# Encoder block on one core: the first four key tiles in one pass over K, weights of the next group cast before the last K step, head norms with a lag of two

## The chip, the core and the metric

The kernel runs on one core of a Trainium2 chip. A core has a matrix engine (TensorE, PE in the profile), VectorE (DVE), ScalarE (ACT), GpSimd (POOL) and SyncE (SP), which here issues nearly all transfers. Each engine works through its own instructions in program order and waits on semaphores for the others. The metric is the time of one execution on the device in microseconds; a time is the median of several executions.

## What is computed

One encoder layer over 1024 tokens of 1024 channels, in float32:

```
h = rms_norm(x, norm1_g)
a, gate, q, k, v = split(h @ w_in)
conv_out = silu(layer_norm(depthwise_conv(a * sigmoid(gate))))
q, k = rms_norm per head of 64 (q), rms_norm per head of 64 (k)
attn_out = neighbourhood_attention(q, k, v, rpb)
x = x + concat(conv_out, attn_out) @ w_out
h = rms_norm(x, norm2_g)
x = x + (silu(h @ w_gate) * (h @ w_up)) @ w_down
```

## The kernel before

The order of the work is written out by hand; no scheduler moves anything. Every large product is taken as three float32r matmuls (`mac`, lines 110 to 114): an operand is split into a rounded high half and the low rest; high by high, high by low and low by high are summed in PSUM. The split of weights is `split` (line 103): ScalarE casts (line 104), POOL or VectorE subtracts (line 108).

Weights come as chunks in a fixed list: wk0 to wk3 (the key projection's four K steps of 256 channels), then ag10, ag00, ag11 and so on for the gated convolution. `issue` (line 134) sends the next chunk from SP into one of three raw buffers, `take` (line 144) splits a chunk, `take_parts` (line 156) hands the split out in pieces.

The input is used transposed: `load_xt` (line 215) brings a quarter of x transposed, for the first or second 256 tokens of a half (FIRST, SECOND) or for all 512, and `h_split` (line 256) scales it by the norm's weight and splits it (ScalarE line 259, VectorE line 260) into hT. The row norm 1/rms itself, r1, is not multiplied in there; `stats1` (line 276) computes it for one tile of 128 tokens, odd tiles by bn_stats on VectorE, even tiles by a square on ScalarE, with a square root on ScalarE and a reciprocal on VectorE behind each. `r_rows` (line 284) spreads r1 of four tiles along rows with four transposes on TensorE (line 289), which the gate and value steps of the convolution group need.

A key tile z1t is 24 matmuls of 128x512. `head_post` (line 420) is what follows it: square (ScalarE, line 368), sum (VectorE, 369), square root (ScalarE, 375), reciprocal (VectorE, 380), scaling (VectorE, 382), and `head_T` (line 386): four transposes on TensorE (389) and a copy to kT on ScalarE (396). head_T is put in a list, `woven`, behind empty entries (seven, line 426); after each `mac` of a later group one entry is taken from the list. `step` (line 408) keeps the post-work of a group until the next group has been issued.

The start of the kernel, lines 505 to 541: tiles 0 and 1 go through the four K steps together, with wk split just ahead; then the second 256 tokens are split, statistics of tiles 0 and 1 follow, then tile 2, statistics of tiles 2 and 3, the split of ag10 (line 533), and tile 3 with the head norms of the tiles before it. Then come r_rows(0) and the groups gl00, gl01 (first half of the tokens) and gl10, gl11 (`glu_step`, line 430).

Of the kernel before, what the change touches and what calls it, by code (L numbers as in the profile page):

```python
# [12 lines left out]
P = 128  # L13
D = 1024
S = 1024
KB = D // P
# [51 lines left out]
def build(ctx, tc, a):  # L68
    nc = tc.nc
    pe, act, dve, pool = nc.tensor, nc.scalar, nc.vector, nc.gpsimd  # L70
# [5 lines left out]
    def T(tag, shape, bufs, name, dt=F32):  # L76
        return sb.tile(shape, dt, tag=tag, bufs=bufs, name=name)

    def G(name, dt=F32):
        return T("G", [P, 1024], 22, name, dt)  # L80

    def R(name):
        return T("R", [P, 1024], 3, name)

    def H(name, dt=F32):
        return T("H", [P, 4096], 6, name, dt)

    def ST(name, dt=F32):
        return T("st", [P, 512], 5, name, dt)

    def SM(name, n=8):
        return T("sm", [P, 8], 16, name)[:, :n]

    def mm(name):
        return ps.tile([P, 512], F32, tag="mm", bufs=4, name=name)

    def tp(name):
        return ps.tile([P, 512], F32, tag="tp", bufs=2, name=name)
# [4 lines left out]
    def split(hi, lo, src, sub=(pool,)):  # L103
        act.copy(hi, src)  # L104
        n = src.shape[-1] // len(sub)
        for i, eng in enumerate(sub):
            sl = slice(i * n, (i + 1) * n)
            eng.tensor_tensor(*[w[..., sl] for w in (lo, src, hi.bitcast(F32))], OP.subtract)  # L108

    def mac(acc, l, r, start, stop):  # L110
        (lh, ll), (rh, rl) = l, r
        pe.matmul(acc, lh, rh, start=start, stop=False, skip_group_check=True)  # L112
        pe.matmul(acc, lh, rl, start=False, stop=False, skip_group_check=True)  # L113
        pe.matmul(acc, ll, rh, start=False, stop=stop, skip_group_check=True)  # L114


    woven = []
# [10 lines left out]
    chunks, raws = [], {}  # L128
    pos = [0, 0]
# [4 lines left out]
    def issue():  # L134
        if pos[0] < len(chunks):
            src, name, _, _ = chunks[pos[0]]
            raws[pos[0]] = R(name + "r")
            d = raws[pos[0]]
            if len(src.shape) == 3:
                d = d.rearrange("p (k m) -> p k m", k=src.shape[1])  # L140
            nc.sync.dma_start(d, src)
            pos[0] += 1

    def take(n=1, ahead=True):
        for _ in range(n):
            i = pos[1]
            while pos[0] <= i:
                issue()
            _, _, dst, sub = chunks[i]
            hi, lo = dst()  # L150
            split(hi, lo, raws.pop(i), sub)
            pos[1] += 1
            if ahead and pos[0] < i + 4:
                issue()
# [22 lines left out]
    wn = {n: [] for n in range(3)}  # L177
# [29 lines left out]
    hT = [[H(f"hT{h}{w}", F32R).rearrange("p (k s) -> p k s", s=512) for w in range(2)] for h in range(2)]  # L207
    x_t, xr = {}, {}
    FIRST, SECOND, ALL = slice(0, 256), slice(256, 512), slice(0, 512)

    def load_x(t):
        x_t[t] = G(f"x{t}")
        nc.sync.dma_start(x_t[t], a["x"][t * P:(t + 1) * P, :])

    def load_xt(h, kp, sl):
        if (h, kp) not in xr:
            xr[h, kp] = G(f"xt{h}{kp}").rearrange("p (k s) -> p k s", s=512)
        nc.sync.dma_start(xr[h, kp][:, :, sl], a["xt"][h, kp][:, :, sl])

    for kp in range(4):  # L220
        load_xt(0, kp, FIRST)
        if kp < 3:
            issue()
    ones = ST("ones")[:, :P]
    ident = T("ident", [P, P], 1, "ident")
    par = T("par", [P, 146], 1, "par")
    nc.scalar.dma_start(par, a["par"])
    g1 = par[:, 0:8]
    dwk = par[:, 8:132].rearrange("p (c t) -> p c t", t=CW)
    dwb, lng, lnb = par[:, 132:136], par[:, 136:140], par[:, 140:144]  # L230
# [3 lines left out]
    warm = SM("warm", 1)  # L234
    act.activation(warm, eps, AF.Sqrt)
    pool.memset(ones, 1.0)
    pool.affine_select(ident, ones, pattern=[[-1, P]], compare_op=OP.is_equal, fill=0.0,
                       base=0, channel_multiplier=1)
    qgs = T("qgs", [P, 1], 1, "qgs")
# [16 lines left out]
    def h_split(h, k, sl):  # L256
        src = xr[h, k // 2][:, k % 2, sl]
        hi, lo = [w[:, k, sl] for w in hT[h]]
        act.activation(hi, src, AF.Copy, scale=g1[:, k:k + 1])
        dve.scalar_tensor_tensor(lo, src, g1[:, k:k + 1], hi.bitcast(F32), OP.mult, OP.subtract)  # L260
# [15 lines left out]
    def stats1(t):  # L276
        ss, scale = (bn_sum if t % 2 else sq_sum)(t)
        sd = SM(f"sd1{t}", 1)
        act.activation(sd, ss, AF.Sqrt, bias=eps, scale=scale)
        dve.reciprocal(r1[:, t:t + 1], sd)  # L280
# [11 lines left out]
    def nat(n, t):  # L292
        z = mm(f"z{n}{t}")
        h, o = divmod(t * P, 512)
        for k in range(KB):
            mac(z, [q[:, k, o:o + P] for q in hT[h]],
                [q[:, (k % 2) * 512:(k % 2) * 512 + 512] for q in wn[n][k // 2]], k == 0, k == KB - 1)
            weave()
        return z
# [56 lines left out]
    def pump(n):  # L356
        for _ in range(n):
            if not next(conv, False):
                return
# [4 lines left out]
    def head_sq(n, t, z):  # L364
        sq, ss = ST(f"sq{n}{t}"), SM(f"s{n}{t}")
        r = r1[:, t:t + 1]
        if n == 1 and t < 4:
            act.activation(sq, z, AF.Square, scale=r)
            dve.tensor_reduce(ss, sq.rearrange("p (h d) -> p h d", d=HD), mybir.AxisListType.X, OP.add)
        else:  # L370
            for h in range(NH):
                act.activation(sq[:, h * HD:(h + 1) * HD], z[:, h * HD:(h + 1) * HD], AF.Square, scale=r,  # L372
                               accum_out=ss[:, h:h + 1])
        sd = SM(f"d{n}{t}")
        act.activation(sd, ss, AF.Sqrt, bias=eps, scale=1.0 / HD)
        return sd

    def head_scale(n, t, z, sd):
        r = SM(f"r{n}{t}")
        dve.reciprocal(r, sd)  # L380
        zn = ST(f"zn{n}{t}")
        dve.scalar_tensor_tensor(zn.rearrange("p (h d) -> p h d", d=HD), z.rearrange("p (h d) -> p h d", d=HD),
                                 r1[:, t:t + 1], r[:, :, None].to_broadcast([P, NH, HD]), OP.mult, OP.mult)
        return zn

    def head_T(n, t, zn):
        pt = tp(f"zt{n}{t}")
        for c in range(4):
            pe.transpose(pt[:, c * P:(c + 1) * P], zn[:, c * P:(c + 1) * P], ident)
        if n == 0:  # L390
            q5 = qT.rearrange("p c (h b i j) -> p c h b i j", h=2, b=4, j=16)
            p5 = pt.rearrange("p (c i b j) -> p c i b j", c=4, i=2, j=16)
            for i in range(2):
                act.activation(q5[:, :, t // 4, :, 2 * (t % 4) + i, :], p5[:, :, i], AF.Copy, scale=qgs)
        else:
            act.activation(kT[:, :, t * P:(t + 1) * P], pt.rearrange("p (c s) -> p c s", s=P), AF.Copy, scale=kg)
# [9 lines left out]
    pend = []  # L406
# [10 lines left out]
            pump(n_taps)  # L417
        side()

    def head_post(n, t, z):  # L420
        def f(n_taps):
            sd = head_sq(n, t, z)
            pump(2 + {(1, 5): 3, (0, 1): 2}.get((n, t), 0))
            zn = head_scale(n, t, z, sd)
            pump(1)
            woven.extend([lambda: None] * 7)
            woven.append(lambda: head_T(n, t, zn))
        return f

# [71 lines left out]
    def project(n, t, post):  # L501
        z = nat(n, t)
        step(post(n, t, z))

    zs = [mm(f"z1{t}") for t in range(2)]
    for kp in range(4):
        parts = []
        take_parts(parts, 2, dve)
        for j in range(2):
            h_split(0, 2 * kp + j, FIRST)  # L510
            parts[j]()
        if kp == 0:
            for q in range(4):
                load_xt(0, q, SECOND)
            load_x(0)
            load_x(1)
        if kp == 2:
            load_x(2)
            load_x(3)
        for j in range(2):  # L520
            for t in range(2):
                k = 2 * kp + j
                mac(zs[t], [q[:, k, t * P:(t + 1) * P] for q in hT[0]],
                    [q[:, j * 512:(j + 1) * 512] for q in wn[1][kp]], k == 0, k == KB - 1)
    for k in range(KB):
        h_split(0, k, SECOND)
    stats1(0)
    stats1(1)
    pend.extend(head_post(1, t, zs[t]) for t in range(2))
    project(1, 2, head_post)  # L530
    stats1(2)
    stats1(3)
    take(1, False)
    for q in range(4):
        load_xt(1, q, ALL)
    project(1, 3, head_post)
    for t in range(4, 8):
        load_x(t)
    take(1)
# [470 lines left out]
    gt, bank, sl, u2, late = {}, {}, {}, {}, []  # L1010
# [205 lines left out]
    for s, p in enumerate(SEQ):  # L1216
        for k in range(QF - 2):
            n = s * QF + k
# [34 lines left out]
```

## Time and profile before

| | us |
|---|---|
| median of 3 runs | 1063.78 (1063.1 to 1064.61) |
| the profiled execution's own time | 1063.23 |
| its span, first to last instruction | 1061.5 |
| TensorE busy | 1045.5 |
| VectorE busy | 703.9 |
| ScalarE busy | 450.9 |
| GpSimd busy | 383.8 |

A row of the timeline gives the start and the length in us, the engine, the line, the operation, what is written and read, and in brackets how long the engine had been idle and what released it. The chain of waits follows the work that ended last back from the end; its rows are start, length, engine and line. The list of waits gives who waited for whom: total us, times, longest.

### The profile page before, as it was taken

To read this page: it belongs to the slowest core of one execution; us is meant where nothing else is said; L and a number is where in the kernel's file an instruction comes from. 1 tells how busy PE (TensorE), PEld (TensorE's weight loads), DVE (VectorE), ACT (ScalarE), POOL (GpSimd) and SP (SyncE) were. 2 spreads that over 40 slices of the span, in tenths; PEclk is the share of its full clock that TensorE was granted. 3 is DMA by queue.
4 is the path that set the end of the run, shared out by engine and by line. 5 is a ranking of instruction groups with operands and counts; after the bars stand their busy time and mean duration, and the time that the engine had idled before them with its cause. 6 is when DMAs were issued, how large, how long until landed. Compare 5 with 4: busy or idle time off the path is not lost.

```text
span 1061.5 us, 14053 instructions
## 1 busy us (share of the span) xinstructions
PE 1045.5 (98%) x5068; PEld 847.8 (80%) x5068; DVE 703.9 (66%) x1055; ACT 450.9 (42%) x987; POOL 383.8 (36%) x301
## 2 busy tenths in 40 slices
PE   7999999999999999999999999999999999999997
PEld 6888888876667887788888888888888888888886
DVE  6788987877765257666465564564655567858883
ACT  6456347726766234532323223232233344433441
POOL 0126765523542302444554544545444200002310
PEclk9999999999999999999999999999999999999999
DMA  9416781245504422032322323232231597634541
GB/s 333 165 49 224 223 256 38 77 151 159 165 30 161 137 100 80 23 127 83 134 96 96 109 99 102 97 129 100 70 134 75 198 320 275 208 99 137 188 141 42
DMA packets 68245, 144.06 MB, mean 136 GB/s; under 512 B 12496, under 2 KB 21200, under 8 KB 67536
## 3 DMA queue, kind: packets, MB, share of 16 engines
q1 hardware_dynamic: 66336, 139.95, 39.2%
q10 hardware_dynamic: 1840, 3.22, 0.9%
q8 instruction: 40, 0.66, 0.3%
q14 instruction: 29, 0.24, 0.1%
HBM read 103.99 MB, written 44.76 MB: 140 GB/s over the span
## 4 chain that ended last, share of the span: by engine, by line
PE 92%; DVE 5%; ACT 1%; issue 0%; DMA 0%; SPq 0%; DVEq 0%; ACTq 0%
PE B L113 5%; PE B L114 5%; PE B L112 5%; PE D L112 4%; PE D L114 4%; PE D L113 4%; PE A L112 4%; PE A L113 3%; PE A L114 3%; PE z L112 3%; PE z L113 3%; PE z L114 3%; PE gl L114 3%; PE gl L112 3%; PE gl L113 3%; DVE cv L319 3%
## 5 line engine op out<-in xcount | busy, mean ns | idle before, releaser
L319 DVE SCALAR_TENSOR_TENSOR cv<-u,par,cv 128x1009 f32<-128x1009 f32 (+14 forms) x92 | 117.5, 1277 | 2.4
L345 POOL TENSOR_TENSOR pa<-pa,pr 128x1022 f32<-128x1022 f32 (+5 forms) x24 | 58.0, 2415 | 50.8 <-ACT pr L344 35.2
L104 ACT CAST op<-sr 128x512 fp32r<-128x512 f32 x77 | 47.7, 619 | 50.2 <-PE B2d L114 21.3
L108 DVE TENSOR_TENSOR op<-sr,op 128x512 fp32r<-128x512 f32 x77 | 58.2, 756 | 14.8 <-ACT op L104 14.8
L1036 DVE TENSOR_TENSOR g<-B,g 128x512 f32<-128x512 f32 x22 | 15.2, 690 | 79.0 <-PE B L114 79.0
L1208 POOL TENSOR_TENSOR ou<-ou,resm 128x512 f32<-128x512 f32 x8 | 13.1, 1651 | 142.7 <-ACT op L104 135.0
L1045 ACT ACTIVATE D<-D 128x512 f32<-128x512 f32 x22 | 12.8, 582 | 112.8 <-DVE D L1044 112.8
L1031 DVE TENSOR_TENSOR u<-B,g 128x512 f32<-128x512 f32 x22 | 15.2, 691 | 62.0 <-PE B L114 62.0
L104 ACT CAST op<-wd 128x512 fp32r<-128x512 f32 x66 | 40.9, 619 | 33.5 <-DVE wd L1123 18.6
L108 DVE TENSOR_TENSOR op<-wd,op 128x512 fp32r<-128x512 f32 x66 | 49.7, 753 | 3.0 <-ACT op L104 1.3
L889 DVE TENSOR_TENSOR ts<-gu,ts 128x512 f32<-128x512 f32 x44 | 51.0, 1159 | 0.8
L633 POOL TENSOR_SCALAR e<-e,rs 128x288 f32<-128x288 f32 (+1 forms) x64 | 34.1, 545 | 45.9 <-DVE rs L631 37.1
L1034 ACT ACTIVATE A<-A 128x512 f32<-128x512 f32 x20 | 11.6, 582 | 76.3 <-PE A L114 76.3
L626 ACT ACTIVATE e<-e,mx 128x288 f32<-128x288 f32 (+1 forms) x64 | 36.2, 569 | 7.3 <-DVE mx L624 7.3
L889 DVE TENSOR_TENSOR ts<-gu 128x512 f32<-128x512 f32 x22 | 33.6, 1528 | 0.0
L624 DVE CUSTOM_DVE_ANT_0 e<-s,tab 128x288 f32<-128x288 f32 (+1 forms) x64 | 29.9, 504 | 3.6 <-PE s L611 3.6
L642 PEld LDWEIGHTS p<-ident,e 128*96 128x96 f32 (+1 forms) x192 | 20.1, 133 | 15.0 <-issue 10.4
L372 ACT ACTIVATE sq<-z,r 128x64 f32<-128x64 f32 x96 | 28.6, 334 | 6.5 <-PE z L114 6.5
L642 PE MATMUL p<-ident,e 128*96 128x128 f32 (+1 forms) x192 | 27.6, 280 | 0.6 <-DVE pT L647 0.6
L658 PE MATMUL o<-pT,vw 96*64 96x128 f32 (+1 forms) x384 | 28.0, 281 | 0.0
L611 PE MATMUL s<-kT,qT 64*128 64x288 f32 (+1 forms) x128 | 27.5, 495 | 0.5 <-DVE mx L624 0.5
L344 ACT ACTIVATE pr<-u,par 128x1022 f32<-128x1022 f32 (+5 forms) x24 | 27.0, 1137 | 1.6 <-ACT vs L402 1.6
(1038 smaller groups left out, 3452.6 us busy)
## 6 DMA issues: line engine op xcount, KB each, us to landing
gu<-in_gu SPq DMA_DIRECT2D x44, 512.0 KB
sr<-sd SPq DMA_DIRECT2D x77, 256.0 KB
sd<-sd SPq DMA_DIRECT2D x22, 512.0 KB
wd<-in_wd SPq DMA_DIRECT2D x44, 256.0 KB
sd<-g SPq DMA_DIRECT2D x33, 256.0 KB
x<-in_x SPq DMA_DIRECT2D x16, 512.0 KB
xd<-x SPq DMA_DIRECT2D x8, 512.0 KB
resm<-xd SPq DMA_DIRECT2D x16, 256.0 KB
```

Source lines behind the costliest of these rows:

```text
L104: act.copy(hi, src)
L108: eng.tensor_tensor(*[w[..., sl] for w in (lo, src, hi.bitcast(F32))], OP.subtract)
L112: pe.matmul(acc, lh, rh, start=start, stop=False, skip_group_check=True)
L113: pe.matmul(acc, lh, rl, start=False, stop=False, skip_group_check=True)
L114: pe.matmul(acc, ll, rh, start=False, stop=stop, skip_group_check=True)
L319: dve.scalar_tensor_tensor(acc[:, o], uc[:, i], dwk[:, c, t:t + 1], acc[:, o], OP.mult, OP.add)
L345: pool.tensor_tensor(pa[:, o], pa[:, o], pr[:, o], OP.add)
L624: dve.tensor_tensor_reduce(out=e[:, hh], in0=ss[hh], in1=tab[rh, cb][2 * hp + hh], scale=-1.0, scalar=3.0e38, op0=OP.add, op1=OP.min, accu ...
L626: act.activation(e[:, hh], e[:, hh], AF.Exp, bias=mx, scale=-1.0, accum_out=rs[:, hh:hh + 1])
L633: pool.tensor_scalar(es[i][:, hh], es[i][:, hh], rs[:, hh:hh + 1], 1.0, op0=OP.mult, op1=OP.mult)
L642: pe.transpose(pt[:m, g * P:(g + 1) * P], es[i][:, hh, g * m:(g + 1) * m], ident)
L889: dve.tensor_tensor(o, l, r, OP.subtract)
```

## The change

The diff, with the loops that it rewrites:

```diff
--- before.py
+++ after.py
@@ -134,11 +134,14 @@
     def issue():
         if pos[0] < len(chunks):
             src, name, _, _ = chunks[pos[0]]
-            raws[pos[0]] = R(name + "r")
+            if pos[0] not in raws:
+                raws[pos[0]] = R(name + "r")
             d = raws[pos[0]]
             if len(src.shape) == 3:
                 d = d.rearrange("p (k m) -> p k m", k=src.shape[1])
-            nc.sync.dma_start(d, src)
+            for q in (0, 1) if name == "wk0" else (None,):
+                sl = slice(None) if q is None else slice(q * 512, q * 512 + 512)
+                (nc.scalar if q == 0 else nc.sync).dma_start(d[:, sl], src[:, sl])
             pos[0] += 1
 
     def take(n=1, ahead=True):
@@ -215,16 +218,20 @@
     def load_xt(h, kp, sl):
         if (h, kp) not in xr:
             xr[h, kp] = G(f"xt{h}{kp}").rearrange("p (k s) -> p k s", s=512)
-        nc.sync.dma_start(xr[h, kp][:, :, sl], a["xt"][h, kp][:, :, sl])
-
+        for ks in (slice(0, 1), slice(1, 2)) if (h, kp, sl) == (0, 0, FIRST) else (slice(0, 2),):
+            nc.sync.dma_start(xr[h, kp][:, ks, sl], a["xt"][h, kp][:, ks, sl])
+
+    xr[0, 0] = G("xt00").rearrange("p (k s) -> p k s", s=512)
+    raws[0] = R("wk0r")
+    ones = ST("ones")[:, :P]
+    ident = T("ident", [P, P], 1, "ident")
+    par = T("par", [P, 146], 1, "par")
+    nc.scalar.dma_start(par, a["par"])
     for kp in range(4):
         load_xt(0, kp, FIRST)
         if kp < 3:
             issue()
-    ones = ST("ones")[:, :P]
-    ident = T("ident", [P, P], 1, "ident")
-    par = T("par", [P, 146], 1, "par")
-    nc.scalar.dma_start(par, a["par"])
+        load_xt(0, kp, SECOND)
     g1 = par[:, 0:8]
     dwk = par[:, 8:132].rearrange("p (c t) -> p c t", t=CW)
     dwb, lng, lnb = par[:, 132:136], par[:, 136:140], par[:, 140:144]
@@ -234,6 +241,10 @@
     warm = SM("warm", 1)
     act.activation(warm, eps, AF.Sqrt)
     pool.memset(ones, 1.0)
+
+    run_up = tp("up")
+    for _ in range(9):
+        pe.matmul(run_up[:, :P], ones, ones, start=True, stop=True)
     pool.affine_select(ident, ones, pattern=[[-1, P]], compare_op=OP.is_equal, fill=0.0,
                        base=0, channel_multiplier=1)
     qgs = T("qgs", [P, 1], 1, "qgs")
@@ -417,13 +428,13 @@
             pump(n_taps)
         side()
 
-    def head_post(n, t, z):
+    def head_post(n, t, z, lag=7):
         def f(n_taps):
             sd = head_sq(n, t, z)
             pump(2 + {(1, 5): 3, (0, 1): 2}.get((n, t), 0))
             zn = head_scale(n, t, z, sd)
             pump(1)
-            woven.extend([lambda: None] * 7)
+            woven.extend([lambda: None] * lag)
             woven.append(lambda: head_T(n, t, zn))
         return f
 
@@ -502,38 +513,41 @@
         z = nat(n, t)
         step(post(n, t, z))
 
-    zs = [mm(f"z1{t}") for t in range(2)]
+    zs = [mm(f"z1{t}") for t in range(4)]
+
+    def four(kp, js, ts):
+        for j, t in ((j, t) for j in js for t in ts):
+            k = 2 * kp + j
+            mac(zs[t], [q[:, k, t * P:(t + 1) * P] for q in hT[0]],
+                [q[:, j * 512:(j + 1) * 512] for q in wn[1][kp]], k == 0, k == KB - 1)
+
     for kp in range(4):
         parts = []
         take_parts(parts, 2, dve)
         for j in range(2):
             h_split(0, 2 * kp + j, FIRST)
             parts[j]()
-        if kp == 0:
-            for q in range(4):
-                load_xt(0, q, SECOND)
-            load_x(0)
-            load_x(1)
-        if kp == 2:
-            load_x(2)
-            load_x(3)
         for j in range(2):
-            for t in range(2):
-                k = 2 * kp + j
-                mac(zs[t], [q[:, k, t * P:(t + 1) * P] for q in hT[0]],
-                    [q[:, j * 512:(j + 1) * 512] for q in wn[1][kp]], k == 0, k == KB - 1)
-    for k in range(KB):
-        h_split(0, k, SECOND)
-    stats1(0)
-    stats1(1)
-    pend.extend(head_post(1, t, zs[t]) for t in range(2))
-    project(1, 2, head_post)
-    stats1(2)
-    stats1(3)
+            h_split(0, 2 * kp + j, SECOND)
+        if kp == 1:
+            for t in range(4):
+                load_x(t)
+        if kp < 3:
+            four(kp, (0, 1), (0, 1))
+            four(kp, (0, 1), (2, 3))
     take(1, False)
+    for t in range(4):
+        if t < 2:
+            stats1(t)
+        if t == 1:
+            for q in (2, 3):
+                stats1(q)
+        four(3, (0, 1), (t,))
+        if t < 3:
+            head_post(1, t, zs[t], 2)(4)
+    pend.append(head_post(1, 3, zs[3], 2))
     for q in range(4):
         load_xt(1, q, ALL)
-    project(1, 3, head_post)
     for t in range(4, 8):
         load_x(t)
     take(1)
```

Part by part. The first xt transfer is sent as two (one per 128 channels) and wk0 as two halves, the first from ScalarE's queue; par is sent before the loop; the SECOND half of each xt quarter is sent right behind its FIRST half and the next weights. Nine products of the tile of ones with itself are put on TensorE ahead of everything. All four tiles of the first half go through the K steps together: K steps 0 to 2 for tiles 0 and 1, then 2 and 3; the last K step tile by tile. Both halves of hT are split inside the K step. ag10 is split (`take(1, False)`) ahead of the last K step. The statistics of tile 0 stand before that tile's last K step; those of tiles 1, 2 and 3 stand before tile 1's last K step, behind the head norm of tile 0. Head norms of tiles 0 to 2 follow each tile at once, with two empty entries in front of each head_T instead of seven; that of tile 3 follows the first gl group, also with two. The four x tiles are requested in K step 1.

## The prediction

> **What bounds the kernel now.** I read the page first, then what TensorE waits for, then the chain that ended last, and at the end the timeline of single engines in the first 50 us.
>
> ```profile
> span 1061.5 us, 14053 instructions
> PE 1045.5 (98%) x5068; PEld 847.8 (80%) x5068; DVE 703.9 (66%) x1055; ACT 450.9 (42%) x987; POOL 383.8 (36%) x301
> ...
> PE z L112 <- ACT wk0h L104: 6.5, 1, 6.5
> PE B L113 <- DVE S L108: 0.9, 1, 0.9
> ```
>
> TensorE is busy for 98% of the span. Of the waits listed for it, one is long: 6.5 us before the first projection matmul; the next is 0.9 us. So only TensorE's own time can pay here: its start, its pace, and any idle time. The chain of waits (start, length, what) at the places that the change touches:
>
> ```profile
> 1.54 4.30 DMA wk0r<-in_qkv
> 5.87 0.63 ACT wk0h L104
> 6.54 0.80 PE z L112
> 7.33 0.73 PE z L113
> 8.06 0.43 PE z L114
> ...
> 11.81 0.24 PE z L114
> 12.05 0.24 PE z L112
> ...
> 31.16 0.44 PE zt L389 x4
> ...
> 32.27 0.23 PE gl L113
> 32.52 0.50 PE gl L114
> ...
> 37.80 0.44 PE zt L389 x4
> 43.74 0.44 PE zt L389 x4
> 49.65 0.44 PE zt L389 x4
> ```
>
> Three readings. First, the start is a transfer (wk0r, until 5.87) and a cast (0.63). Second, the first twelve matmuls take 12.05 - 6.54 = 5.51 us, 0.43 each once they follow one another; the next 84 take 31.16 - 12.05 = 19.11, 0.2275 each. The pace doubles some 5 us after TensorE began. At the fast pace, with the one wait for the low half (wk0l is written at 6.52 + 0.69, below, so the second matmul starts 0.72 behind the first), twelve would take 0.72 + 10 x 0.2275 + 0.39 (a single one to its end) = 3.4, so 2.1 us are lost to the slow pace. Third, between 31.16 and 50.09 (49.65 + 0.44) TensorE runs transposes and three gl groups without a hole, except that the first L114 is 0.27 longer than its neighbours.
>
> **The change, edit by edit.** After the third gl group and its transposes the order on every engine is that of before, so I find when TensorE has done that work (50.09 before) and carry the difference to the end. Does the end follow? At 196.88 the chain leaves TensorE for VectorE's convolution taps, but a transpose on TensorE releases that stretch, and it moves with it:
>
> ```profile
> 196.88 0.45 PE zt L389 x4
> ...
> 201.23 0.75 DVE zn L382
> 201.98 1.19 DVE cv L319
> ```
>
> *Start.* Now 128 KB of xt and, on ScalarE's queue, half of wk0 (256 KB) suffice for the first matmul.
>
> ```profile
> 0.78 0.20 POOL L236 MEMSET ones<- 128x128 f32 x1 [0.29 <-POOLq L1243]
> ...
> 4.17 0.51 ACT L259 ACTIVATE hT<-xt,par 128x256 fp32r<-128x256 f32 x1 [1.45 <-DMA xt<-in_xt]
> ...
> 8.37 0.51 ACT L259 ACTIVATE hT<-xt,par 128x256 fp32r<-128x256 f32 x1 [0.96 <-DMA xt<-in_xt]
> ...
> 9.64 0.62 ACT L104 CAST wk1h<-wk1r 128x512 fp32r<-128x512 f32 x1 [0.77 <-DMA wk1r<-in_qkv]
> ```
>
> xt and par (329 KB) had landed at 4.17, wk0r (841 KB in all) at 5.87. Between these the new half lands: bounds of the first matmul 4.17 + 0.67 = 4.8 and 6.54 (0.67 is 6.54 - 5.87). With 457 to 585 KB ahead of its end the line between gives 4.6 to 5.0, plus 0.67: I take 5.4, a gain of 1.1.
>
> *Run-up.* Nine f32 products of ones, free to start when ones is written (0.98). Four f32 transposes of 128 columns take 0.44, so one pass 0.11, and 0.21 at the slow pace (0.43/0.2275 = 1.9). An f32 product may be one or two passes: in the row below 384 matmuls are counted where the code issues 192.
>
> ```profile
> L658 PE MATMUL o<-pT,vw 96*64 96x128 f32 (+1 forms) x384 | 28.0, 281 | 0.0
> ```
>
> So nine need 1.9 to 3.8 us and end before 5.0: they delay nothing. If the pace again doubles 5 us after the first matmul (now 1.1), it does so at 6.1, and 0.7 us of real work runs slow: 0.3 lost instead of 2.1. Bounds: nothing lost, or all 2.1 again (if this work does not count). I take 0.3, because with two passes TensorE is almost as continuously busy as in the row it is nearest to. On this the Trainium skill ("TensorE: Matmul & The Clock Gate", Part 1) says that the clock is doubled after a busy window of about 3.4 us whose phase is free; the trace's 5 us fits one to two such windows, and by the rule 0 to 1.3 us of real work time would be lost.
>
> *Four tiles per K step.* The same 96 matmuls and 16 h_splits in another order. Each K step now lasts 24 x 0.2275 = 5.46 on TensorE instead of 2.73.
>
> ```profile
> 4.71 0.48 DVE L260 SCALAR_TENSOR_TENSOR hT<-xt,par,hT 128x256 fp32r<-128x256 f32 x1 [1.72 <-ACT hT L259]
> ...
> 6.52 0.69 DVE L108 TENSOR_TENSOR wk0l<-wk0r,wk0h 128x512 fp32r<-128x512 f32 x1 [1.33 <-ACT wk0h L104]
> ```
>
> VectorE has four h_splits and two halves of weights per step, 4 x 0.48 + 2 x 0.69 = 3.3, hidden under 5.46. Transfers: SP now sends the second xt halves between the weights. The bytes that had landed at 8.37 (1,097 KB) are now the second half of xt00; its split is done on VectorE a microsecond later, 9.4, and TensorE reaches it at 5.4 + 0.72 + 11 x 0.2275 + 0.3 = 8.9 for its high, 9.4 for its low half. wk1 is 256 KB further back than at 9.64, about 0.85 (512 KB in 1.7 us above), so 10.5, cast by 11.1; TensorE gets there at 11.9. I take 0.3 for both, bounds 0 and 0.8. The later weights lie further ahead of their use.
>
> *ag10 cast before the last K step.* The subtraction on POOL no longer ends with TensorE waiting at 32.52: a gain of 0.27. On ScalarE the cast now stands ahead of tile 0's statistics, which are due only when z10 is done, two K steps after the ones that the weights before ag10 serve.
>
> *Statistics and head norms.* This is where I expect the loss. r1 of tiles 1, 2, 3 stands in program order, on ScalarE and on VectorE, behind the whole head norm of tile 0, and that needs z10. The transposes of r_rows(0) stand on TensorE directly behind z13, in front of the first gl matmul, and need r1 of all four tiles. Let T be the end of z10: on TensorE 18 matmuls are left, 18 x 0.2275 = 4.1 us. The other chain, with the same instructions in the trace:
>
> ```profile
> 19.81 1.27 DVE L266 BATCH_NORM_STATS2 sb<-x 128x6 f32<-128x512 f32 x2
> ...
> 21.61 0.29 ACT L279 ACTIVATE sd<-s,eps 128x1 f32<-128x1 f32 x1 [1.91 <-DVE s L268]
> 21.81 0.67 ACT L368 ACTIVATE sq<-z,r 128x512 f32<-128x512 f32 x1
> ...
> 24.47 0.68 DVE L369 TENSOR_REDUCE s<-sq 128x8 f32<-128x512 f32 x1
> ...
> 25.39 1.01 ACT L273 ACTIVATE j<-x 128x1024 f32<-128x1024 f32 x1
> ...
> 26.96 1.27 DVE L266 BATCH_NORM_STATS2 sb<-x 128x6 f32<-128x512 f32 x2
> ...
> 28.77 0.29 ACT L279 ACTIVATE sd<-s,eps 128x1 f32<-128x1 f32 x1 [1.91 <-DVE s L268]
> ...
> 29.09 0.16 DVE L280 RECIPROCAL r<-sd 128x1 f32<-128x1 f32 x1 [0.36 <-ACT sd L279]
> ```
>
> Head norm of tile 0, from sq to VectorE's next instruction: 24.47 - 21.81 = 2.66. Tile 1, bn_stats to sd: 21.61 - 19.81 = 1.80, and 0.20 to ScalarE's next. Tile 2, square to the next bn_stats: 26.96 - 25.39 = 1.57. Tile 3, bn_stats to sd 1.81, to the reciprocal 0.32, which takes 0.16. Sum 8.52, and 0.05 for the first semaphore: T + 8.6. TensorE stands idle for 8.6 - 4.1 = **4.5 us**.
>
> What is late next: tile 1's sq follows sd of tile 3 (T + 8.3), its head norm ends at T + 10.95, and there tile 2's reduce begins. From that reduce to the end of tile 3's zn the order is that of before:
>
> ```profile
> 32.93 0.69 DVE L369 TENSOR_REDUCE s<-sq 128x8 f32<-128x512 f32 x1 [3.67 <-ACT sq L368]
> ...
> 35.55 4.37 DVE L260 SCALAR_TENSOR_TENSOR hT<-xt,par,hT 128x512 fp32r<-128x512 f32 x4
> ...
> 41.12 0.75 DVE L382 SCALAR_TENSOR_TENSOR zn<-z,r,r 128x512 f32<-128x512 f32 x1
> ```
>
> 41.87 - 32.93 = 8.94, so zn13 is there at T + 19.9. With a lag of 2 its transposes now stand after four K steps of the second gl group. TensorE gets there at 8.6 + 0.6 (rb) + 24 x 0.23 + 3 x 0.44 (three transposes) + 12 x 0.23 = T + 18.8 and waits **1.1 us** more. Before, that transpose stood at the end of the third group with time to spare. Then come 0.6 (0.44 and the pipeline's tail), 12 matmuls (2.8) and the third group (49.65 - 44.18 = 5.5): T + 28.8.
>
> T = 5.4 + 0.72 + 0.39 (a matmul to its end) + 76 x 0.2275 + 0.3 + 0.3 = 24.4. So 53.2 against 50.1: **+3.1 us**. By terms: start -1.1, pace -1.8, ag10 -0.3, supply +0.3, the two waits +5.6, and 0.4 for the tail of the pipeline behind each wait and rounding.
> The profiled execution took 1063.23 (1.7 around the span), so the sum is 1066.3; the median shown, 1063.78, lies 0.55 higher and the three runs spread over 1.5, which the phase of the pace change alone could make. So 2.5 over the median.
>
> **The rivals.** (a) *The slow pace comes back.* TensorE idles 4.5 us in one piece, and no wait in the trace but the first (6.5) is over 0.9, so no row shows what such a hole does; at the start the idle engine was slow. Price: 5 us at half pace, 2.5, of which the second wait hides its 1.1: +1.4, 1067.7. The Trainium skill (same page, Part 1) states that an idle window of about 3.4 us halves the clock, which no run so far shows; by it this would come in those phases where a window fits into the hole.
> (b) *The run-up does not count*, so that part of the change does not do what it says: twelve slow matmuls again, +1.8, 1068.1.
> (c) *No second wait*: if the four hT splits, of which the first overlaps POOL's subtraction (4.37 for four, where the last three have 0.66 each), run 1.1 shorter, zn13 is in time: 1065.2.
> (d) *The other side, faster:* r1 of tile 3 is ready when z13 is. It decides at 4.1 us after T; then rb follows at once and the third group ends at T + 4.1 + 0.44 + 2 x 5.5 + 4 x 0.44 + 5.5 = T + 22.8, 47.2 in all: 2.9 gained, 1060.3. For it speaks that these statistics need nothing but x, which is requested in the second K step; against it that each engine runs in program order, and the 8.6 is made of rows with hardly a gap in them.
>
> **How the numbers follow.** Forecast 0.45, (a) 0.18, (b) 0.17, (c) 0.12, (d) 0.08. Predicted 1066.3. Within the forecast the start, the supply and the pace leave about 0.8 each way. The range 1064.6 to 1069.0 takes in (a), (b) and (c), and leaves out (d) and some of the worst phases of (b) with (a). A measurement of this kernel can tell about 0.2%, 2.1 us, from no change: over 1065.9 is slower. That has (a), (b) and two thirds of the forecast: 0.65; the rest of it and (c) are the same, 0.27; (d) is faster, 0.08.
>
> **What would show it.** In the waits of TensorE: rb on the reciprocal of r1, 4 to 5 us, once; zt on zn, about 1 us, once; the first z matmul 5.4 instead of 6.5 after the start. In the chain of waits: z matmuls at 0.23 from about 6 us on; a stretch ACT sq, DVE zn, DVE sb, ACT j, DVE sb, ACT sd, DVE r between z and rb; gl matmuls behind it at 0.23, or 0.43 if (a). Wrong it would be if rb follows z13 at once, or if the time to the third group's end is not handed on to the end of the span.

## The result and the profile after

| | before | changed |
|---|---|---|
| median of 6 runs each, us | 1063.24 (1062.38 to 1064.61) | 1066.48 (1066.0 to 1068.19) |
| ratio, with its 95% interval | | 1.003 (1.002 to 1.0041) |
| the profiled execution's own time | 1063.23 | 1068.19 |
| its span | 1061.5 | 1066.5 |

The changed kernel is slower by 3.2 us. The profiled execution is the longest of the six, so a second profile of the same kernel, of an execution of 1066.01, stands beside it below. First a line of the page of the profiled execution of 1068.19 (busy time of each engine), then its list of TensorE's waits in the first 60 us (total, times, longest) and the row of the run-up:

```profile
PE 1051.4 (99%) x5086; PEld 852.4 (80%) x5086; DVE 704.6 (66%) x1055; ACT 451.0 (42%) x987; POOL 383.0 (36%) x301
```

```profile
PE rb L300 <- DVE r L291: 3.8, 3, 1.9
PE up L247 <- POOL ones L243: 1.0, 1, 1.0
PE z L112 <- ACT wk0h L104: 0.5, 1, 0.5
```

```profile
1.04 4.21 PE L247 MATMUL up<-ones 128*128 128x128 f32 x18 [1.04 <-POOL ones L243]
```

The 6.5 us at the start have become 1.0 and 0.5 around the run-up, the first z matmul starts at 5.7, and a wait that was not there before has come: rb, the transposes of r_rows(0), on the reciprocals of r1, three times, 3.8 us. Busy time of TensorE has risen by 5.9 us. The 18 matmuls of the run-up take 4.2 of them; the other 1.7 are a first sign that matmuls went at a slower pace somewhere. The chain of waits shows where (start, length, what):

```profile
9.79 0.43 PE z L114
10.22 0.38 PE z L112
10.60 0.23 PE z L113
...
25.80 0.24 PE z L114
...
26.07 0.70 ACT sq L379
...
28.08 0.75 DVE zn L393
28.83 1.20 DVE sb L277 x2
...
30.56 0.29 ACT sd L290
30.86 1.05 ACT j L284 x2
...
32.42 1.20 DVE sb L277 x2
...
34.46 0.17 DVE r L291
...
34.68 0.47 PE rb L300
35.15 0.43 PE gl L112
...
38.01 0.23 PE gl L113
...
38.95 0.68 DVE rb L301
...
43.97 0.61 DVE s L380
...
44.90 1.24 ACT hT L270 x2
46.13 0.63 PE zt L400 x4
```

z10 is done at 26.05. From there the chain leaves TensorE: square and head norm of tile 0, then statistics of tiles 1, 2 and 3, and only at 34.68 the last transpose of rb, 8.6 us after z10. TensorE had the other three tiles done at 26.05 + 4.1 = 30.1. The gl matmuls behind the hole take 0.43 each until 38.0, then 0.23. A little later the chain leaves TensorE once more, for VectorE and ScalarE, and comes back at 46.13 with the head transposes of tile 3: it is the head norm of this tile, not TensorE, that sets that time (zn13 ends at 45.98). The windows view of the same execution (per window: length, busy time and number of instructions on PE, PEld, DVE, ACT and POOL, then the granted clock, DMA share and GB/s) shows that the 0.43 goes with the clock:

```profile
34.00:35.00 1.00, 0.32 (x2) 0.32 (x3) 0.26 (x2) 0.87 (x2) 0.00 (x0) 0.66 0.89 352
35.00:36.00 1.00, 1.00 (x4) 0.81 (x4) 0.69 (x1) 0.25 (x3) 0.00 (x0) 0.50 0.30 123
...
37.00:38.00 1.00, 1.00 (x4) 0.78 (x3) 0.67 (x2) 0.29 (x2) 0.00 (x0) 0.64 0.02 8
38.00:39.00 1.00, 1.00 (x9) 0.82 (x8) 0.93 (x3) 1.00 (x3) 0.00 (x0) 1.00 0.00 0
```

The 0.66 between 34 and 35 is half the clock for the last 0.68 us of that window, and the 0.64 between 37 and 38 is half the clock for its first 0.72: the granted clock falls to 0.50 at about 34.3, while TensorE still waits for the last transpose, and comes back at about 37.7, after 3.4 us. The Trainium skill ("TensorE: Matmul & The Clock Gate", Part 1) names half the clock as the state after an idle window of about 3.4 us; the trace agrees with the half, 0.50, but TensorE was not idle that long in one piece: three single transposes lie in the hole, and the longest wait is 1.9 us. The 3.4 us measured here are those of the slow stretch itself.

In this execution the first matmuls also went at 0.43, until 10.6. In the second profile (timeline: start, length, engine, line, operation) they did not:

```profile
5.67 0.50 PE L112 MATMUL z<-wk0h,hT 128*128 128x512 f32 x1 [0.42 <-ACT wk0h L104]
6.39 0.50 PE L113 MATMUL z<-wk0l,hT 128*128 128x512 f32 x1 [0.23 <-DVE wk0l L108]
6.74 0.40 PE L114 MATMUL z<-wk0h,hT 128*128 128x512 f32 x1
...
23.77 0.39 PE L114 MATMUL z<-wk3h,hT 128*128 128x512 f32 x1
...
32.81 0.47 PE L300 MATMUL rb<-ident,r 128*128 128x128 f32 x1 [1.89 <-DVE r L291]
...
43.85 0.39 PE L114 MATMUL gl<-hT,ag00l 128*128 128x512 f32 x1
44.26 0.63 PE L400 MATMUL zt<-ident,zn 128*128 128x128 f32 x4
```

Matmuls start 0.23 to 0.35 apart from the second on, z10 is done at 24.16 (23.77 + 0.39) instead of 26.05, rb again 8.6 us later, and the transposes of tile 3 (44.26) come 20.1 us after z10, as in the first profile (46.13 - 26.05). These 1.9 us are nearly all of the 2.2 by which the two executions differ.

### The profile page after: what moved, and what is told of

The parts are those of the page before. It is cut to its first block, busy times and chain, and to the rows that moved or that the text cites. A ratio compares the mean times of both kernels' runs of the same rounds, so it can differ in the third digit from the quotient of the medians.

```text
span 1066.5 us, 14092 instructions
## 1 busy us (share of the span) xinstructions
PE 1051.4 (99%) x5086; PEld 852.4 (80%) x5086; DVE 704.6 (66%) x1055; ACT 451.0 (42%) x987; POOL 383.0 (36%) x301
## 4 chain that ended last, share of the span: by engine, by line
PE 91%; DVE 6%; ACT 2%; issue 1%; DMA 0%; ACTq 0%; DVEq 0%
PE B L113 5%; PE B L114 5%; PE B L112 5%; PE D L114 4%; PE D L113 4%; PE D L112 4%; PE A L112 3%; PE A L113 3%; PE A L114 3%; PE z L112 3%; PE z L113 3%; PE z L114 3%; DVE cv L330 3%; PE gl L112 3%; PE gl L114 3%; PE gl L113 3%
## 5 line engine op out<-in xcount | busy, mean ns | idle before, releaser
L656 PEld LDWEIGHTS p<-ident,e 128*96 128x96 f32 (+1 forms) x192 | 20.1, 133 | 15.0 <-issue 10.4
```

What stands on the lines that cost most here:

```text
L656: pe.transpose(pt[:m, g * P:(g + 1) * P], es[i][:, hh, g * m:(g + 1) * m], ident)
```

## The experiments

Each is timed in five rounds beside the kernel before. The medians of the kernel before in the three batches are 1063.2 (the first four rows), 1063.8 (the next four) and 1063.4 (the last three); where two experiments of different batches are compared, differences under about 0.6 us mean little.

| | median, us | ratio to before (95%) |
|---|---|---|
| statistics first | 1061.57 | 0.9985 (0.9976 to 0.9994) |
| lag 7 for tile 3 | 1066.72 | 1.0038 (1.0025 to 1.005) |
| no run-up | 1068.05 | 1.0047 (1.0034 to 1.0059) |
| run-up in bfloat16 | 1065.90 | 1.0029 (1.0018 to 1.0041) |
| lag 7, hole filled | 1064.39 | 1.0009 (0.9999 to 1.0018) |
| start undone | 1069.78 | 1.0056 (1.0043 to 1.0068) |
| one root, lag 7, bfloat16 run-up | 1059.87 | 0.9966 (0.9954 to 0.9979) |
| before, with start and run-up | 1061.87 | 0.9987 (0.9978 to 0.9996) |
| the same, bfloat16 run-up | 1062.29 | 0.9990 (0.9982 to 0.9999) |
| lag 2, hole filled | 1065.88 | 1.0026 (1.0017 to 1.0035) |
| changed kernel again | 1066.42 | 1.0026 (1.0016 to 1.0035) |

**Statistics first.**

```diff
     for t in range(4):
-        if t < 2:
-            stats1(t)
-        if t == 1:
-            for q in (2, 3):
+        if t == 0:
+            for q in range(4):
                 stats1(q)
         four(3, (0, 1), (t,))
```

> The statistics of all four tiles stand ahead of tile 0's last K step instead of behind its head norm. Theory: rb waited for r1 of tile 3 (4.5 us of idle TensorE) and zt13 was late by 1.1 us because of it. Both go: about 5.4 us less than the changed kernel (1066.5), so 1061.1, some 2.1 us below the kernel before (1063.2); the list of waits has no rb of over 0.5 us, and the pace behind rb stays at 0.23 a matmul. Rival: the loss lies in the start (transfers in halves, four tiles per K step): then 1065 to 1066.5 remains. Rival: the hole only moves, because z11 to z13 then wait for something else on VectorE: 1063 to 1066.

Measured 1061.57, 4.9 below the changed kernel, and faster than the kernel before. All eleven runs lie between 1061.22 and 1062.18. The list of waits in the first 70 us:

```profile
PE zt L400 <- ACT hT L270: 1.0, 1, 1.0
...
PE gl L112 <- DVE zn L393: 0.4, 1, 0.4
```

The rb wait is gone, and in the windows of this profile the granted clock stays at 1.00 between z and gl. The transposes of tile 3 come at 40.05, 15.8 us after z10 instead of 20.1. So the place of four statistics is what made the change slow. The expectation was wrong in one point: the wait for tile 3's transposes does not go with the late statistics, 1.0 of it stays, for TensorE and the head norms now both run earlier. A wait that it did not have is the first gl matmul on zn10 (0.4). The four key tiles hold all four buffers of the PSUM tag mm; the first gl group needs the one of z10, and zn10 is the last to read it.

**Lag 7 for tile 3.**

```diff
-    pend.append(head_post(1, 3, zs[3], 2))
+    pend.append(head_post(1, 3, zs[3], 7))
```

> Tile 3's head transposes get a lag of seven again, the rest is the changed kernel. Theory: zt13 is a second wait of up to 1.1 us, so 1065.4 where TensorE comes out of the hole at full pace, and no zt wait in the list. Rival: the profile shows 0.43 a matmul for some 3 us behind the hole; that uses up the 1.1 us already, so lag 7 saves only 0.2 and the time stays at 1066.3.

Measured 1066.72: nothing gained, the rival's case. Behind the hole TensorE is slower, so it comes to tile 3's transposes later, when zn13 is there; the second profile above has 44.26 - 43.85 - 0.23 = 0.2 of wait left.

**Lag 7, hole filled.** TensorE gets useless work in the hole; r1 is as late as before.

```diff
     take(1)
+    hole = tp("hole")
+    for _ in range(18):
+        pe.matmul(hole[:, :P], ident, ident, start=True, stop=True)
     r_rows(0)
```

> As the kernel with lag 7 for tile 3, and in the hole before r_rows(0) TensorE runs eighteen float32 products of the identity (some 4.4 us at the full pace); r1 is as late as before. Theory: the half pace behind the hole (0.43 a matmul for 3 us, in every profile that has the hole) comes from TensorE idling; filled, the gl matmuls go at 0.23 at once and the time is 1.3 us less than with lag 7 alone: 1066.7 - 1.3 = 1065.4. Rival: the pace falls for another reason (what the gl matmuls read, or the many transposes): 1066.7 stays, or rises by what the fill delays rb.

Measured 1064.39, 2.3 below lag 7 alone (2.9 when each is taken against the kernel before of its batch), and the granted clock stays at 1.00 in the windows of this profile. The rival is out. The timelines of TensorE, first with lag 7 alone, then with the hole filled:

```profile
32.80 0.32 PE L300 MATMUL rb<-ident,r 128*128 128x128 f32 x1 [1.88 <-DVE r L291]
...
36.34 0.87 PE L400 MATMUL zt<-ident,zn 128*128 128x128 f32 x4
36.97 0.47 PE L112 MATMUL gl<-hT,ag10h 128*128 128x512 f32 x1
```

```profile
28.27 4.18 PE L556 MATMUL hole<-ident 128*128 128x128 f32 x36
...
33.00 0.32 PE L300 MATMUL rb<-ident,r 128*128 128x128 f32 x1 [0.22 <-DVE r L291]
...
35.24 0.60 PE L400 MATMUL zt<-ident,zn 128*128 128x128 f32 x4
35.59 0.48 PE L112 MATMUL gl<-hT,ag10h 128*128 128x512 f32 x1
```

From the last rb to the gl matmul behind the first transposes it is 4.17 us without and 2.59 with the fill: 1.6 us for the half pace. That is also what the two profiled executions differ by (1066.19 and 1064.63). Work that computes nothing makes the kernel faster, because the clock is kept. The medians lie further apart; what the rest is, no profile shows.

**Lag 2, hole filled.** The same fill in the changed kernel as it is.

> The changed kernel with its lag of two, and the eighteen products in the hole. Theory: the second wait (zt13 on zn13, 1.1 us) is real but covered by the half pace behind the hole; with the hole filled the pace stays full and the wait comes into view: a zt wait of about 1 us in the list, and 1.1 us more than with lag 7 and fill (1064.4), 1065.5. Rival: zn13 is in time, 1064.4 as with lag 7.

Measured 1065.88, 1.5 above lag 7 with fill. Its list of waits now has the second wait; below it are the last matmul of z10 and the transposes in the timeline:

```profile
PE zt L400 <- ACT hT L270: 1.2, 1, 1.2
```

```profile
23.73 0.39 PE L114 MATMUL z<-wk3h,hT 128*128 128x512 f32 x1
...
44.22 0.63 PE L400 MATMUL zt<-ident,zn 128*128 128x128 f32 x4 [1.19 <-ACT hT L270]
```

So the second wait is real, 1.2 us. The releaser in the row is the one the profile names; zn13 ends just before, at 44.07. The transposes start 44.22 - 24.12 = 20.1 us after z10, at full pace and with the wait; in the changed kernel it was 20.1 too, at half pace and with hardly a wait. What sets this time in both is zn13, and the half pace only uses up what TensorE would have waited. The two profiled executions take the same time, 1065.96 and 1066.01.

**No run-up.** The nine products and their tile are left out.

> Without the nine products of ones, the rest is the changed kernel. Theory: they count in part of the executions (the six times of the changed kernel fall at 1066.0 to 1066.8 and at 1068.0 to 1068.2): without them nearly all executions are slow for some 5 us, 1068 in the median, none near 1066. Rival: they do not count at all (in the profile the pace doubled 9.4 us after the first of them and 4.7 us after the first real matmul), and the two values are the phase of the clock alone: median and spread stay, 1066 to 1068.2.

Measured 1068.05, all five runs within 1067.94 to 1068.15. Its chain of waits has twelve slow matmuls again (the first at 5.58):

```profile
10.52 0.43 PE z L113
10.95 0.29 PE z L114
11.24 0.23 PE z L112
```

So the run-up counts: 1.6 us in the median, though not in every execution (the profiled one of the changed kernel, 1068.19, is as if it had none).

**Run-up in bfloat16.**

```diff
-    for _ in range(9):
-        pe.matmul(run_up[:, :P], ones, ones, start=True, stop=True)
+    for _ in range(10):
+        pe.matmul(run_up, ones_b[:, :P], ones_b, start=True, stop=True)
```

(ones_b is a bfloat16 view of a tile of 256 float32 ones.)

> The run-up as ten bfloat16 products of 512 columns on the same tile instead of nine float32 ones of 128: it lasts as long, but streams one column a cycle without loads between. Theory: the float32 run-up counts only in part because TensorE is not dense enough in it; then all executions are at the fast pace before 6 us: 1066.0 or a little less in all five, spread under 1 us. Rival: density does not matter, only the phase against the run-up's 4.2 us: the same two values as the changed kernel.

Measured 1065.90; four of six between 1065.77 and 1065.96, the others 1066.66 and 1067.13. No value at 1068 is among them, but the spread is over 1 us, and among the ten later executions of the changed kernel with its float32 run-up (the last experiment) there is none at 1068 either. So this does not show that the wider run-up is better, nor that density matters. (The trace has a weight load in front of each of the ten products, so "without loads between" does not hold.)

**Start undone.** The wk0 transfer, on SP's queue, and the first xt transfer are whole again.

> wk0 goes as one transfer from SP and the first xt quarter as one, all else is the changed kernel. Theory: the split start brings the first matmul from 6.54 to 5.7; undone, everything moves by some 0.8 us: 1067.3. Rival: the end of the run-up is then a microsecond further from the first real matmul, so that it counts less often: 1068 to 1069. Rival: the start does not set the end, 1066.5.

Measured 1069.78, 3.3 above the changed kernel, in a batch in which the kernel before was 0.5 higher: more than the later start. The timeline of TensorE:

```profile
6.49 0.50 PE L112 MATMUL z<-wk0h,hT 128*128 128x512 f32 x1 [1.49 <-ACT wk0h L104]
7.22 0.50 PE L113 MATMUL z<-wk0l,hT 128*128 128x512 f32 x1 [0.23 <-DVE wk0l L108]
7.56 0.39 PE L114 MATMUL z<-wk0h,hT 128*128 128x512 f32 x1
7.79 0.43 PE L112 MATMUL z<-wk0h,hT 128*128 128x512 f32 x1
8.02 0.62 PE L113 MATMUL z<-wk0l,hT 128*128 128x512 f32 x1
```

The first real matmuls go at the full pace (0.23 apart), then at 8.0 the pace falls to 0.43. The run-up had counted, and 1.5 us after the first real matmul the pace was lost again. Before that matmul TensorE had waited 1.5 us; in the profiles that kept the pace this wait is 0.9 at most. So the first rival, that the run-up counts less often, comes nearest, and split start and run-up hang together; that the gap alone is the cause is argued from this one profile. The profiled execution (1068.56) is the fastest of the five, and what the others lost on top is not shown.

**Before, with start and run-up alone,** and then the same with the bfloat16 run-up: two tiles per K step, statistics and head norms as before.

> The kernel before with the split start (wk0 in halves on two queues, xt in two, par first) and the nine products of ones alone; two tiles per K step, statistics and head norms as before. Theory: start 0.8 and pace 2 us are gained, but two tiles use a K step's weights up in 2.7 us and the weights come 3.5 to 4 us apart, so TensorE waits for wk1 and wk2, over 1 us: 1061.5 (the four tiles per K step are worth that). Rival: the weights are in time, four tiles per K step are worth nothing: 1060.3.

> The kernel before with the split start and the wide bfloat16 run-up (the profile of the run with the float32 one fell on a slow start, 0.43 a matmul until 9.9 us, and so could not show a wait for weights). Theory: at the full pace two tiles use up a K step in 2.7 us, faster than the weights come, and TensorE waits 1 to 1.5 us in all for wk1 and wk2; the time stays at 1061.5 to 1062, and the list of waits has z on wk1h or wk1l. So four tiles per K step are worth what is left to 1059.9. Rival: no such wait, 1060.3 or less.

Measured 1061.87 and 1062.29: near the times of the two theories, but not by their mechanism. In the profile of the first the matmuls come 0.43 apart until 9.9 us, and it shows no wait for weights; it is the fastest of its eleven executions all the same (1061.52). The second runs at the full pace from 6.7 us, and its waits are:

```profile
PE gl L114 <- POOL ag10l L108: 1.6, 1, 1.6
...
PE z L113 <- DVE wk1l L108: 0.2, 1, 0.2
```

and the first of them in TensorE's timeline:

```profile
29.90 0.39 PE L113 MATMUL gl<-hT,ag10h 128*128 128x512 f32 x1
31.85 0.50 PE L114 MATMUL gl<-hT,ag10l 128*128 128x512 f32 x1 [1.56 <-POOL ag10l L108]
```

The weights cost less than expected (three matmuls around 9.1 to 10.2 start 0.34, 0.72 and 0.34 apart, 0.7 us lost), and wk2 nothing. The greater wait is one that no expectation had: the low half of ag10, 31.85 - 29.90 - 0.23 = 1.7 us. By these rows four tiles per K step and the early cast of ag10 cover 2.4 us, but only when TensorE comes there early. In each of the two kernels two of eleven executions are some 2 us longer than the rest, with the float32 run-up as with the bfloat16 one.

**One root, lag 7, bfloat16 run-up.** The changed kernel with the statistics early and under one root, the lag of seven for tile 3, and the run-up in bfloat16 as above (that part of the edit, and the lines of the old statistics that go, are left out here).

```diff
+        if t == 0:
+            ss = SM("s10", 4)
+            for q in (1, 3):
+                bn_sum(q, ss[:, q:q + 1])
+            for q in (0, 2):
+                act.activation(cv(f"j{q}"), x_t[q], AF.Square, scale=D ** -0.5, accum_out=ss[:, q:q + 1])
+            act.activation(ss, ss, AF.Sqrt, bias=eps)
+            dve.reciprocal(r1[:, :4], ss)
         four(3, (0, 1), (t,))
...
-    pend.append(head_post(1, 3, zs[3], 2))
+    pend.append(head_post(1, 3, zs[3], 7))
```

> The statistics of the four tiles ahead of tile 0's last K step, with the two sums of VectorE and the two of ScalarE side by side and one square root and one reciprocal for all four; lag 7 for tile 3; the run-up in bfloat16, 512 columns. Theory: the kernel with early statistics (1061.6) still had TensorE waiting 0.4 us for zn10, whose PSUM bank the first gl group needs, and 1.0 us for zt13; both go, and the wider run-up takes away the rest of the slow starts: 1060.1, 3 us below the kernel before. Rival: x of tile 3 lands too late for one common root, zn10 comes later than before: 1061 to 1062.

Measured 1059.87 (1059.61 to 1060.41), 0.34% below the kernel before in the same batch, as the theory had it. Three things were changed at once, so what each is worth is not shown by this run alone. In the first 60 us TensorE's list of waits has a single row:

```profile
PE up L249 <- POOL ones L245: 1.1, 1, 1.1
```

**The changed kernel again.**

> The changed kernel as it is, beside the other two on one chip, for a second profile. Theory: where the run-up counts, the first real matmuls go at 0.23 at once and z10 is done near 24 us instead of 26; the hole of 4.5 us, the half pace behind it and the time of 1066.0 follow. Rival: the faster executions differ in the hole or behind it, and z10 is again done at 26.

Measured 1066.42 (1065.64 to 1067.5). The profile is the second one shown with the result; the theory holds.

## Why the prediction was right, and where it was not

The predicted time, 1066.3, and the sign were right, and so was the path that sets the time: the statistics behind the head norm of tile 0 make zn13 late, and TensorE can't get to the end of the second gl group before. Forecast was zn13 at T + 19.9; it ends 19.95 behind z10 in both profiles, and the third gl group, forecast to end at 53.2, ends at about 53.1 in the second profile (44.26 + 0.63, twelve matmuls of 0.23 and a group of 5.5). What TensorE does ahead of that point was forecast wrongly. Point by point:

- *Start.* 5.4 forecast, 5.6 to 5.9 measured. The gain is 0.6 to 0.9 instead of 1.1.
- *Run-up.* Forecast 0.3 us lost. Measured nothing lost in the second profile and some 1.9 in the first: both bounds occur. Its worth, 1.8 by rival (b), is 1.6 by the run without it.
- *Supply of weights.* Forecast 0.3; z10 ends at 24.2 against 24.1 worked out without it, 0.1. The start came 0.3 later than forecast, supply and run-up cost 0.5 less; that T came out near the 24.4 forecast is in part luck.
- *The hole.* r1 of tile 3 forecast at T + 8.6, rb measured at 8.6 behind z10 in both profiles; 4.5 us of hole. The run with the statistics first shows that this is the cause. But the prediction has TensorE idle "in one piece" and one wait of 4 to 5 us: each of the four transposes waits for its own r1, so three of them lie in the hole, and the list has three waits, 3.8 in all.
- *The second wait.* Forecast 1.1. It is 1.2 where the pace stays full (lag 2, hole filled), but 0.2 in the changed kernel. Rival (c), no second wait, is out.
- *Half pace behind the hole.* The forecast left it out and gave it to rival (a), with 0.18; it came in every profile that has the hole. So the mechanism of the rival is there, but not its price of 1.4 us. The rival took 5 us at half pace, 2.5; it is 3.4 us, and 1.6 by the two timelines with lag 7. And the second wait takes up more of it: with the half pace and without, tile 3's transposes start 20.1 us after z10. That this cost nothing in the profiled executions is luck, and narrow: only 0.2 us of the wait is left, and with a lag of seven, where that wait is gone, the half pace alone makes the kernel as long. In the medians the changed kernel is 0.5 above the one with the hole filled (1066.42 and 1065.88), because five of its ten executions lie at 1066.8 to 1067.5; the other five, at 1065.6 to 1066.0, are as fast as nine of the eleven with the fill. Whether the half pace makes those five long is open; none of them was profiled.
- *ag10.* Sized at 0.27 from the trace before. In the kernel before with the new start it is 1.7: TensorE gets to that point 2.2 us earlier (29.90 against 32.10), the subtraction on POOL begins only 0.6 earlier (29.44 against 30.08). In the changed kernel it does not enter the time, for there the subtraction is done by 21.6, long before.
- *Rival (d), 1060.3.* With the statistics first 1061.57 was measured. The 1.4 us of waits left (bank of z10, zt13) are about the difference; the kernel without them, and with the bfloat16 run-up, takes 1059.87.
- *Handing on to the end.* 53.1 - 50.1 = 3.0 us at the third group, 1066.01 - 1063.23 = 2.8 at the end.

## What to carry to other kernels

When work on the engine that sets the time is regrouped, look for what a small instruction on that engine, in program order, needs from the others, and follow that chain instruction by instruction on the engines' own order: here four 0.1 us transposes cost 4.5 us because statistics that needed only the input were queued behind a norm that needed the matmuls. A hole costs more than its length if it lowers the clock, and less if another wait lies behind it; so price waits in sequence, not one by one, and look for the one path that sets the time at the point where they meet. A gain at the start moves every later deadline: a subtraction that came 0.27 us late becomes a wait of 1.7.

## What the runs showed of the hardware

The half pace needs no idle stretch of 3 us: the longest wait in the hole is 1.9 us, with single transposes of 0.3 us between, and in the run with the start undone it came after a gap of 1.5 us soon after the run-up. In all six profiles that have the hole (the changed kernel twice, lag 7 alone, no run-up, run-up in bfloat16, start undone) the granted clock is at 0.50 for 3.4 us, and so it is in the run with the start undone from 8.0 to 11.4. But this stretch does not begin at one place: it began 0.4 us before the last transpose of r_rows(0) in the first profile, and 0.7 behind it, after two gl matmuls at full pace, in the profile with lag 7 alone. Whether single transposes count as work for the clock, no run shows. At the start of the kernel the granted clock in the windows view reads 1.00 while matmuls come 0.43 apart (the profiled execution of the changed kernel, 6 to 10 us); behind the hole it reads 0.50 at the same 0.43. So a slow start is read from the distance of the matmuls, not from that column.
